# One hybrid encoder layer on one core: transposes as plain matmuls, an affine delta state, head sums in other PSUM banks, modulation sums ordered later

## The chip, the cores and the metric

The kernel runs on one core of one Trainium2 chip. The metric is the device time of one execution in microseconds (us), lower is better. A core has TensorE (PE: matmuls, with a separate row PEld for its weight loads), VectorE (DVE), ScalarE (ACT), GpSimd (POOL) and SyncE (SP, which only issues DMAs here). Each of them takes its instructions strictly in the order of the program. That order is written by a compile-time scheduler, which walks a model of the machine in time, takes the instruction of highest priority that is ready, and hands out buffers.

## The reference

One inference step of one layer (depth 1, width 1024) for two groups of rows that share the weights: 1024 prompt rows and 64 sample rows with caches.

```python
mod = (silu(c) @ w_ada + b_ada).reshape(B, 6, 1, 1024)      # shift1 scale1 gate1 shift2 scale2 gate2
h = rms_norm(x, norm_mix) * (1 + scale1) + shift1
u = h @ w_in                                                # 2568 columns, split into four mixers
mix = concat([conv(u), gated_deltanet(u), pool(u), stick_breaking(u)]) @ w_out
x = x + gate1 * mix
h2 = rms_norm(x, norm_ffn) * (1 + scale2) + shift2
x = x + gate2 * ((silu(h2 @ w_gate) * (h2 @ w_up)) @ w_down)
```

The gated DeltaNet works in chunks of 64 rows with one 64x64 state S for each of 4 heads. Inside a group of chunks, with everything that does not depend on S ready (u, w, attn, q, k per chunk):

```python
def step(S, xs):
    u_i, w_i, attn_i, q_i, k_i, gl = xs
    v_new = u_i - w_i @ S
    o = q_i @ S + attn_i @ v_new
    S = S * gl + k_i.T @ v_new
```

The stick-breaking mixer normalises its queries and keys per head (a sum of squares over the 64 columns of a head) before its attention.

## The kernel before

Rows are processed feature-major (features on partitions) in two halves: HA, prompt rows 0 to 511, and HB, prompt rows 512 to 1023 plus the 64 sample rows, 576 columns in two chunks of 288. For each half the program traces, in this order: `norm1`, `in_proj` (the input projection), `mixers`, `out_proj`, `ffn`. The last lines of the kernel (1166 to 1178) trace `in_proj(HA)`, `norm1(HB)`, `mixers(HA)`, `in_proj(HB)`, the rest of the modulation sums, `mixers(HB)`, `out_proj(HA)`, `ffn(HA)`, `out_proj(HB)`, `ffn(HB)`. Program order is the scheduler's priority, so PE fills what earlier parts leave free with later parts. Parts inside `tc.high_priority()` (evacuations of PSUM, norms, weight loads) come first.

Projections. Every product with a weight is done in single-pass fp32r on split operands: `load_w` (line 318) loads 512 KB of weights, ACT rounds them to `whi`, DVE subtracts to `wlo`; `gemm_fm` (340) runs three matmuls (hi*hi, hi*lo, lo*hi) per k tile into one PSUM bank per chunk, from `gemm_bank` (335). While `wide[0]` is false that is the pool `mm` with two banks. `in_proj` runs `sb_vab` (values of the attention), `gemm_out` for the DeltaNet columns, `sb_qk` (keys and queries, four tiles k0 k1 q0 q1), then `gemm_out` for the conv (4 tiles) and pool (2 tiles) columns. Results go to DRAM through buffers `ST` (four in all). HA and HB share the modulated inputs `hi`, `lo`, and `out_proj(HA)` loads the mixers' output `mixd` into the same buffers, in the order of slices 6, 7, 4, 5, 0, 1, 2, 3 (2 and 3 are the DeltaNet's, written as `mixA<-kbe`).

Head sums. `sb_qk` (393) copies a tile out of PSUM, squares it into `qksq`, and multiplies the squares by a block-diagonal of ones (`pqk`, line 407). The bank of `pqk` is `PC`, a pool of a single bank. `PC` is also the bank of the conv's means and variances (`pmu`, `pvar`, lines 901 and 914) and of the pool's product (`ppl`, 1016).

DeltaNet. `delta` (856) runs two groups of four chunks per half and for HB one more group of one chunk (the sample rows). Products of 64x64 blocks sit at partitions 0 to 63 and 64 to 127: `batch` (713) issues 2 pairs x chunks x 2 such matmuls, 16 in a full group. `flip` (721) transposes blocks: the lower half (hp = 0) by PE's transpose instruction (line 728), the upper half by a plain matmul with an identity. A full group has four flips: `pkt`, `pvt`, `pw0` (shown as `pw` with the operand `cst`), `pof`. The triangular inverse goes through POOL and four DRAM round trips; its result comes back as `X<-xd`. The state loop (lines 822 to 841) does for each chunk: `pvn` = w S and q S into `po`, DVE `vn`, two ACT scalings of S, `pkv` = k vn and attn vn into `po`, DVE S += `pkv`.

Modulation sums. The 16 rows of shift1 and scale1 are done at the start. The 32 others (gate1, shift2, scale2, gate2) are one DVE reduction each over a 128x1024 tile of `w_ada` (`ada_dve`, 209), once per row group. For the prompt `ada_step` (245) loads the tile into one of two buffers `g0`, `g1` (the FFN's later `th`, `tl`), behind the last weight load traced, and reduces it. `ADA_N` = 1 step is traced per projection tile of HA (12 tiles in `sb_qk` and `gemm_out`), `ADA_B` = 2 per tile of HB; line 1171 traces what is left. So 12 steps stand in HA and the other 20 in the first ten tiles of HB. `scale2` (260) needs the first 24; the last 8 (gate2) are read by the FFN's `residual`. For the sample rows `ada_sample` (253) does 32 more.

Of the kernel before, what the change touches and what calls it, by code (L numbers as in the profile page):

```python
# [7 lines left out]
F32 = mybir.dt.float32  # L8
F32R = mybir.dt.float32r
I32 = mybir.dt.int32  # L10
ACTF = mybir.ActivationFunctionType
ALU = mybir.AluOpType
# [10 lines left out]
SILU_T = 14  # L23
DEFER = 2
SHIFT_DVE = (3, 6)
ADA_N = 1
ADA_B = 2
WIDE = 6
KT = 8
FT = 22  # L30
# [29 lines left out]
def hybrid_encoder_kernel(ctx: ExitStack, tc: tile.TileContext, io):  # L60
    nc = tc.nc
    P = 128
# [39 lines left out]
    def PC(name):  # L102
        return ps_cv.tile([P, 512], F32, tag="cv", name=name)
# [9 lines left out]
    def act_(out, in_, func, bias=0.0, scale=1.0):  # L113
        nc.scalar.activation(out, in_, func, bias=bias, scale=scale)  # L114

    def copy_a(out, in_):
        nc.scalar.activation(out, in_, ACTF.Copy)  # L117
# [4 lines left out]
    def tt(out, a, b, op):  # L122
        nc.vector.tensor_tensor(out=out, in0=a, in1=b, op=op)  # L123
# [13 lines left out]
    def mm(out, lhsT, rhs, start=True, stop=True):  # L137
        return nc.tensor.matmul(out, lhsT=lhsT, rhs=rhs, start=start, stop=stop)  # L138

    def mms(out, lhsT, rhs, start=True, stop=True):  # L140
        nc.tensor.matmul(out, lhsT=lhsT, rhs=rhs, start=start, stop=stop, skip_group_check=True)  # L141
# [10 lines left out]
    def C(name):  # L152
        o, w = CONST_COLS[name]
        return cst[:, o:o + w]
# [53 lines left out]

    def ada_dve(w, col, groups):
        for g in groups:  # L210
            junk = sb.tile([P, 1024], mybir.dt.bfloat16, tag="pl", name="junk")
            nc.vector.tensor_tensor_reduce(out=junk, in0=w, in1=cbt[g], scale=1.0, scalar=V("b_ada", col),  # L212
                                           op0=ALU.mult, op1=ALU.add, accum_out=mod[:, col, g:g + 1])

# [30 lines left out]
    def ada_step(n=1):  # L245
        for _ in range(min(n, len(ada_left))):
            j = ada_left.pop(0)
            t = gp.tile([P, 1152], F32, tag=f"g{j % 2}", name="wadt")
            with behind():
                nc.sync.dma_start(out=t[:, 0:1024], in_=io["wadat"][j])  # L250
            ada_dve(t[:, 0:1024], 16 + j, (0,))
# [83 lines left out]
    def gemm_bank(name="pg"):  # L335
        turn[0] += 1
        pool, tag = BANKS[turn[0] % 8] if wide[0] else BANKS[0]
        return pool.tile([P, 512], F32, tag=tag, name=name)
# [54 lines left out]
    def sb_qk(h):  # L393
        n_ = h.n
        for pi, piece in enumerate(("k", "q")):
            for m in range(2):
                ada_step(ADA_B if h.samp else ADA_N)
                t, sq = ST("qk"), ST("qksq")
                lo = ST("qkl") if piece == "k" else t
                tiles = gemm_fm(h, io["wfm"][14 + 2 * pi + m], h.hi, h.lo, KALL)  # L400
                with tc.high_priority():
                    for ps, c0, n in tiles:
                        copy_a(t[:, c0:c0 + n], ps[:, 0:n])
                        act_(sq[:, c0:c0 + n], ps[:, 0:n], ACTF.Square)
                    for c0, n in h.chunks:
                        pn = PC("pqk")
                        mm(pn[:, 0:n], C("bdones"), sq[:, c0:c0 + n])
                        act_(sq[:, c0:c0 + n], pn[:, 0:n], ACTF.Ln, bias=epst, scale=1.0 / 64)
                    act_(sq[:, 0:n_], sq[:, 0:n_], ACTF.Exp, scale=-0.5)
                    stt(t[:, 0:n_], t[:, 0:n_], gqk[:, pi:pi + 1], sq[:, 0:n_], ALU.mult, ALU.mult)  # L410
                    copy_a(sq[:, 0:n_].bitcast(F32R), t[:, 0:n_])
                    d = sbd[piece, h.name]
                    if piece == "k":
                        nc.sync.dma_start(out=io["sbk"][m, :, h.row0:h.row0 + n_], in_=t[:, 0:n_])
                    tt(lo[:, 0:n_].bitcast(F32R), t[:, 0:n_], sq[:, 0:n_], ALU.subtract)
                    for x, v in enumerate((sq, lo)):
                        if piece == "k":
                            for y in range(2):
                                nc.sync.dma_start(out=d[2 * m + y, 64 * x:64 * x + 64], in_=v[64 * y:64 * y + 64, 0:n_])
                        else:  # L420
                            nc.sync.dma_start(out=d[128 * m:128 * m + 128, x], in_=v[:, 0:n_])
# [265 lines left out]
    def dn_group(h, feats, gate, D, ch0, nch, tok0, mtok0, S):  # L687
# [7 lines left out]
        def v4(t):  # L695
            return t[:, 0:w].rearrange("p (a c d) -> p a c d", a=2, c=nch)
# [10 lines left out]
        def PS(name):  # L707
            return PD(name)
# [12 lines left out]
        def flip(out, lhs):  # L721
            for pair in range(2):
                for c in range(nch):
                    j = (pair * nch + c) * 64
                    for hp in range(2):
                        r = slice(64 * hp, 64 * hp + 64)
                        if hp == 0:
                            nc.tensor.transpose(out[r, j:j + 64], lhs(pair, c, j)[r], C("sel2")[r, 0:64])
                        else:
                            mm(out[r, j:j + 64], lhs(pair, c, j)[r], C("sel2")[r, 0:64])  # L730

        blk = lambda t: (lambda pair, c, j: t[:, j:j + 64])
        ft = lambda i: (lambda pair, c, j: ftok(i, pair, c))
# [83 lines left out]
        batch(pwt, blk(kbe), blk(Y))  # L817
        wT = T4("X")
        copy_a(wT[:, 0:w], pwt[:, 0:w])
        po = ps_dn.tile([P, 512], F32, tag="dn", name="po")  # L820
        u4, o4 = v4(u), v4(po)
        for c in range(nch):
            pv2 = PS("pvn")
            for pair in range(2):
                j = (pair * nch + c) * 64
                for hp in range(2):
                    r = slice(64 * hp, 64 * hp + 64)
                    mm(pv2[r, pair * 64:pair * 64 + 64], wT[r, j:j + 64], S[r, pair])
                    mms(po[r, j:j + 64], qd[r, j:j + 64], S[r, pair], c == 0 and pair == 0, False)
            vn = dn.tile([P, 2, 64], F32, tag="vn", name="vn", bufs=2)  # L830
            tt(vn, u4[:, :, c], pv2[:, 0:128].rearrange("p (a d) -> p a d", a=2), ALU.subtract)
            for pair in range(2):
                act_(S[:, pair], S[:, pair], ACTF.Copy, scale=D["gl"][:, pair, ch0 + c:ch0 + c + 1])
            pk2 = PS("pkv")
            for pair in range(2):
                j = (pair * nch + c) * 64
                for hp in range(2):
                    r = slice(64 * hp, 64 * hp + 64)
                    mm(pk2[r, pair * 64:pair * 64 + 64], kup[r, j:j + 64], vn[r, pair])
                    mms(po[r, j:j + 64], at[r, j:j + 64], vn[r, pair], False, True)  # L840
            tt(S, S, pk2[:, 0:128].rearrange("p (a d) -> p a d", a=2), ALU.add)
        sq = T4("Y")
        act_(sq[:, 0:w], po[:, 0:w], ACTF.Square)
        ss = sm.tile([P, 2, 4], F32, tag="oss", name="oss")
# [323 lines left out]
    norm1(HB)  # L1168
    mixers(HA)
    in_proj(HB)  # L1170
    while ada_left:
        ada_step()
    scale2(0)
    mixers(HB)
    out_proj(HA)
    ffn(HA)
    out_proj(HB)
    ffn(HB)
# [176 lines left out]
```

## Time and profile before

| | us |
|---|---|
| three timed runs | 1528.47, 1529.11 (median), 1538.52 |
| profiled execution, whole | 1532.56 |
| its span in the trace | 1530.8 |
| PE busy, DVE busy, ACT busy in the span | 1459.6, 1030.5, 663.2 |

The profiled execution was 1.8 us longer than its span and 3.4 us longer than the median. Times in the views are counted from the start of the span. "Busy" PE time has modelled ends (matmuls are pipelined), so a busy PE is not PE at its peak rate. An engine with `q` (SPq, POOLq) is its sequencer, which issues DMAs. In a row of the timeline the columns are start, duration, engine, line, operation, out<-in, shape, count, and in brackets the idle time before it and what ended it.

### The profile page before, as it was taken

To read this page: it belongs to the slowest core of one execution; us is meant where nothing else is said; L and a number is where in the kernel's file an instruction comes from. 1 tells how busy PE (TensorE), PEld (TensorE's weight loads), DVE (VectorE), ACT (ScalarE), POOL (GpSimd) and SP (SyncE) were. 2 spreads that over 40 slices of the span, in tenths; PEclk is the share of its full clock that TensorE was granted. 3 is DMA by queue.
4 is the path that set the end of the run, shared out by engine and by line. 5 is a ranking of instruction groups with operands and counts; after the bars stand their busy time and mean duration, and the time that the engine had idled before them with its cause. 6 is when DMAs were issued, how large, how long until landed. Compare 5 with 4: busy or idle time off the path is not lost.

```text
span 1530.8 us, 24538 instructions
## 1 busy us (share of the span) xinstructions
PE 1459.6 (95%) x9688; PEld 1259.9 (82%) x9688; DVE 1030.5 (67%) x1816; ACT 663.2 (43%) x1191; POOL 88.3 (6%) x196
## 2 busy tenths in 40 slices
PE   7899999958998989999999999999999999999999
PEld 5777799835896857677878778789899999999998
DVE  7877999865379997666766588744655555555554
ACT  4446554645454567466676442222432222222221
POOL 0000400030003000200300000000000000000000
PEclk7999999968897999699999999999999999999999
DMA  8796677432354213252323477622322222222222
GB/s 287 262 295 208 207 223 236 121 75 90 117 178 145 70 45 93 82 153 84 107 91 91 131 268 260 210 95 86 135 70 84 83 83 84 83 83 84 83 84 103
DMA packets 106867, 205.41 MB, mean 134 GB/s; under 512 B 39360, under 2 KB 49024, under 8 KB 106752
## 3 DMA queue, kind: packets, MB, share of 16 engines
q1 hardware_dynamic: 99936, 193.36, 39.1%
q0 software_dynamic: 6816, 10.49, 3.1%
q8 instruction: 76, 1.25, 0.3%
q14 instruction: 39, 0.32, 0.1%
HBM read 175.57 MB, written 28.24 MB: 133 GB/s over the span
## 4 chain that ended last, share of the span: by engine, by line
PE 70%; issue 11%; DMA 7%; DVE 6%; POOL 3%; ACT 2%; SPq 1%; DVEq 0%; POOLq 0%; ACTq 0%
PE pg L138 59%; PE psC L141 2%; POOL fst L135 1%; POOL fsu L135 1%; PE pw L138 1%; DVE junk L212 1%; PE psO L141 1%; PE z L141 1%; DVE wlo L123 1%; DMA out_sbk_dram<-qk 1%; DMA wadt<-in_wadat_dram 1%; DMA X<-xd 1%; DMA fsn<-nld 1%; DVE xA L126 1%; DVE nrm L126 1%
## 5 line engine op out<-in xcount | busy, mean ns | idle before, releaser
L138 PE MATMUL pg<-hi,whi 128*128 128x288 f32 (+1 forms) x1504 | 504.8, 336 | 7.6 <-ACT vf L117 3.3
L138 PE MATMUL pg<-hi,wlo 128*128 128x288 f32 (+1 forms) x1504 | 500.6, 334 | 4.8 <-DVE wlo L123 4.8
L138 PE MATMUL pg<-lo,whi 128*128 128x288 f32 (+1 forms) x1504 | 502.5, 334 | 1.7 <-DVE lo L126 1.6
L117 ACT ACTIVATE whi<-wraw 128x1024 fp32r<-128x1024 f32 (+2 forms) x192 | 199.7, 1041 | 488.2 <-PE pg L138 422.4
L138 PEld LDWEIGHTS pg<-hi,whi 128*128 128x128 f32 x1504 | 287.1, 191 | 35.5 <-ACT vf L117 4.1
L138 PEld LDWEIGHTS pg<-hi,wlo 128*128 128x128 f32 x1504 | 286.4, 191 | 29.9 <-DVE wlo L123 6.8
L138 PEld LDWEIGHTS pg<-lo,whi 128*128 128x128 f32 x1504 | 287.2, 191 | 27.9 <-issue 3.3
L123 DVE TENSOR_TENSOR wlo<-wraw,whi 128x1024 fp32r<-128x1024 f32 (+2 forms) x192 | 230.9, 1203 | 106.6 <-ACT whi L117 105.4
L138 PE MATMUL pg<-g,whi 128*128 128x288 f32 (+1 forms) x1056 | 253.1, 332 | 0.1
L138 PEld LDWEIGHTS pg<-g,whi 128*128 128x128 f32 x1056 | 180.0, 190 | 14.8 <-ACT acc L114 0.6
L138 PE MATMUL pg<-g,wlo 128*128 128x288 f32 (+1 forms) x528 | 173.1, 331 | 0.0
L126 DVE SCALAR_TENSOR_TENSOR xs<-pg,mod,xs 128x288 f32<-128x288 f32 (+2 forms) x288 | 106.5, 413 | 85.7 <-PE pg L138 82.5
L138 PEld LDWEIGHTS pg<-g,wlo 128*128 128x128 f32 x528 | 100.1, 190 | 7.8
L123 DVE TENSOR_TENSOR fa<-fa,pg 128x288 f32<-128x288 f32 (+1 forms) x66 | 35.0, 531 | 101.4 <-PE pg L138 98.2
L126 DVE SCALAR_TENSOR_TENSOR cy<-cvb,vec,cy 128x512 f32<-128x512 f32 (+1 forms) x120 | 94.2, 799 | 0.2
L126 DVE SCALAR_TENSOR_TENSOR xA<-pg,mod,xA 128x512 f32<-128x512 f32 x96 | 70.6, 747 | 22.8 <-PE pg L138 22.6
L212 DVE CUSTOM_DVE_ANT_0 junk<-wads,cb,vec 128x1024 bf16<-128x1024 f32 x32 | 41.0, 1282 | 17.6 <-DMA wads<-in_wadat_dram 12.8
L114 ACT ACTIVATE e<-e 128x512 f32<-128x512 f32 (+4 forms) x100 | 51.9, 519 | 0.8
L212 DVE CUSTOM_DVE_ANT_0 junk<-wadt,cb,vec 128x1024 bf16<-128x1024 f32 x32 | 41.0, 1282 | 16.3 <-DMA wadt<-in_wadat_dram 16.2
L138 PE MATMUL pg<-mixs,whi 128*128 128x288 f32 x256 | 50.9, 295 | 0.0
L114 ACT ACTIVATE zs<-zs 128x512 f32<-128x512 f32 (+4 forms) x50 | 25.7, 514 | 36.8 <-DVE zs L123 35.7
L138 PEld LDWEIGHTS pg<-mixs,whi 128*128 128x128 f32 x256 | 41.0, 188 | 0.1
(304 smaller groups left out, 1922.7 us busy)
## 6 DMA issues: line engine op xcount, KB each, us to landing
wraw<-in_wgate_dram SPq DMA_DIRECT2D x44, 512.0 KB, 3.7
wraw<-in_wup_dram SPq DMA_DIRECT2D x44, 512.0 KB, 3.8
wraw<-in_wdown_dram SPq DMA_DIRECT2D x44, 512.0 KB, 3.6
wadt<-in_wadat_dram SPq DMA_DIRECT2D x32, 512.0 KB, 5.0
wads<-in_wadat_dram SPq DMA_DIRECT2D x32, 512.0 KB, 4.5
wraw<-in_wfm_dram SPq DMA_DIRECT2D x30, 512.0 KB, 4.3
wraw<-in_wout_dram SPq DMA_DIRECT2D x16, 512.0 KB, 3.7
xA<-in_xa_dram SPq DMA_DIRECT2D x16, 256.0 KB, 6.7
```

What stands on the lines that cost most here:

```text
L114: nc.scalar.activation(out, in_, func, bias=bias, scale=scale)
L117: nc.scalar.activation(out, in_, ACTF.Copy)
L123: nc.vector.tensor_tensor(out=out, in0=a, in1=b, op=op)
L126: nc.vector.scalar_tensor_tensor(out, a, s, b, op0, op1)
L135: nc.gpsimd.tensor_tensor(out=out, in0=a, in1=b, op=op)
L138: return nc.tensor.matmul(out, lhsT=lhsT, rhs=rhs, start=start, stop=stop)
L141: nc.tensor.matmul(out, lhsT=lhsT, rhs=rhs, start=start, stop=stop, skip_group_check=True)
L212: nc.vector.tensor_tensor_reduce(out=junk, in0=w, in1=cbt[g], scale=1.0, scalar=V("b_ada", col), op0=ALU.mult, op1=ALU.add, accum_out=mod[ ...
```

## The change

- `flip`: both halves become plain matmuls with the identity.
- The state loop becomes an affine map. With w itself (`pww`; before, only its transpose `pwt` was made), M = gl I - k^T w is made for all chunks at once (`pmt`, `mt_`), and S_next = k^T u + M S is accumulated in one bank per chunk (`pst`) and copied out by ACT. The states of all chunks are kept in `Sc`; `pvn`, `vn` and `po` are then done for all chunks at once.
- `pqk` takes its bank from `gemm_bank` instead of `PC`.
- `ADA_N` = 0, `ADA_B` = 1: no sums in HA, one per tile in HB (18). The loop after `in_proj(HB)` goes on until 8 are left (6 more), and the last 8 stand after `out_proj(HA)` with high priority.
- A reduction for one row group writes its unused product over its own operand instead of the bf16 buffer `pl`.

```diff
-ADA_N = 1
-ADA_B = 2
+ADA_N = 0
+ADA_B = 1
     def ada_dve(w, col, groups):
         for g in groups:
-            junk = sb.tile([P, 1024], mybir.dt.bfloat16, tag="pl", name="junk")
+            junk = w if len(groups) == 1 else sb.tile([P, 1024], mybir.dt.bfloat16, tag="pl", name="junk")
...
                     for c0, n in h.chunks:
-                        pn = PC("pqk")
+                        pn = gemm_bank("pqk")
                         mm(pn[:, 0:n], C("bdones"), sq[:, c0:c0 + n])
...
                     for hp in range(2):
                         r = slice(64 * hp, 64 * hp + 64)
-                        if hp == 0:
-                            nc.tensor.transpose(out[r, j:j + 64], lhs(pair, c, j)[r], C("sel2")[r, 0:64])
-                        else:
-                            mm(out[r, j:j + 64], lhs(pair, c, j)[r], C("sel2")[r, 0:64])
+                        mm(out[r, j:j + 64], lhs(pair, c, j)[r], C("sel2")[r, 0:64])
...
-        po = ps_dn.tile([P, 512], F32, tag="dn", name="po")
-        u4, o4 = v4(u), v4(po)
+        pw2 = PS("pww")
+        batch(pw2, blk(Y), blk(kbe))
+        wt_ = T4("W")
+        copy_a(wt_[:, 0:w], pw2[:, 0:w])
+        gi = T4("vb")
+        tt(v4(gi), bc(D["gl"]), C("sel2")[:, 0:64].unsqueeze(1).unsqueeze(1).to_broadcast(sh4), ALU.mult)
+        pm = PS("pmt")
+        batch(pm, blk(wt_), blk(kup))
+        mt_ = T4("Y")
+        tt(mt_[:, 0:w], gi[:, 0:w], pm[:, 0:w], ALU.subtract)
+        Sc = T4("kbe")[:, 0:128 * nch].rearrange("p (c a d) -> p c a d", c=nch, a=2)
+        copy_a(Sc[:, 0], S)
+
+        def each(c):
+            for pair in range(2):
+                for hp in range(2):
+                    yield pair, slice(64 * hp, 64 * hp + 64), (pair * nch + c) * 64
...
         for c in range(nch):
-            pv2 = PS("pvn")
-            for pair in range(2):
-                j = (pair * nch + c) * 64
-                for hp in range(2):
-                    r = slice(64 * hp, 64 * hp + 64)
-                    mm(pv2[r, pair * 64:pair * 64 + 64], wT[r, j:j + 64], S[r, pair])
-                    mms(po[r, j:j + 64], qd[r, j:j + 64], S[r, pair], c == 0 and pair == 0, False)
-            vn = dn.tile([P, 2, 64], F32, tag="vn", name="vn", bufs=2)
-            tt(vn, u4[:, :, c], pv2[:, 0:128].rearrange("p (a d) -> p a d", a=2), ALU.subtract)
-            for pair in range(2):
-                act_(S[:, pair], S[:, pair], ACTF.Copy, scale=D["gl"][:, pair, ch0 + c:ch0 + c + 1])
-            pk2 = PS("pkv")
-            for pair in range(2):
-                j = (pair * nch + c) * 64
-                for hp in range(2):
-                    r = slice(64 * hp, 64 * hp + 64)
-                    mm(pk2[r, pair * 64:pair * 64 + 64], kup[r, j:j + 64], vn[r, pair])
-                    mms(po[r, j:j + 64], at[r, j:j + 64], vn[r, pair], False, True)
-            tt(S, S, pk2[:, 0:128].rearrange("p (a d) -> p a d", a=2), ALU.add)
+            pS = PS("pst")
+            for pair, r, j in each(c):
+                mms(pS[r, pair * 64:pair * 64 + 64], kup[r, j:j + 64], u[r, j:j + 64], pair == 0, False)
+            for pair, r, j in each(c):
+                mms(pS[r, pair * 64:pair * 64 + 64], mt_[r, j:j + 64], Sc[r, c, pair], False, True)
+            nxt = S if c == nch - 1 else Sc[:, c + 1]
+            copy_a(nxt, pS[:, 0:128].rearrange("p (a d) -> p a d", a=2))
+        pv2 = PS("pvn")
...
+        vn = T4("W")
+        tt(vn[:, 0:w], u[:, 0:w], pv2[:, 0:w], ALU.subtract)
+        po = PS("po")
...
     in_proj(HB)
-    while ada_left:
+    while len(ada_left) > 8:
         ada_step()
     scale2(0)
     mixers(HB)
     out_proj(HA)
+    with tc.high_priority():
+        while ada_left:
+            ada_step()
     ffn(HA)
```

## Rows read from the trace of the kernel before

**Rows 1.** The page: engines over the span; the chain that ended last, by engine.
```profile
PE 1459.6 (95%) x9688; PEld 1259.9 (82%) x9688; DVE 1030.5 (67%) x1816; ACT 663.2 (43%) x1191; POOL 88.3 (6%) x196
PE 70%; issue 11%; DMA 7%; DVE 6%; POOL 3%; ACT 2%; SPq 1%; DVEq 0%; POOLq 0%; ACTq 0%
```

**Rows 2.** Busy time by stretch: us; PE, PEld, DVE, ACT, POOL; PEclk, DMA share, GB/s.
```profile
150.00:250.00 100.00, 98.89 (x867) 86.42 (x866) 94.06 (x180) 50.22 (x105) 18.31 (x33) 0.97 0.73 220
285.00:380.00 95.00, 71.90 (x656) 49.41 (x657) 61.18 (x126) 51.49 (x111) 14.91 (x36) 0.80 0.28 74
380.00:457.00 77.00, 72.72 (x532) 66.81 (x530) 40.00 (x74) 38.72 (x81) 1.73 (x3) 0.91 0.47 150
457.00:560.00 103.00, 93.81 (x650) 71.58 (x649) 97.51 (x156) 55.10 (x101) 16.12 (x34) 0.88 0.34 101
700.00:900.00 200.00, 199.33 (x1027) 158.66 (x1027) 134.19 (x214) 122.95 (x228) 20.22 (x42) 1.00 0.39 113
```

**Rows 3.** Timeline of ACT: squares of HB's first key tile; logarithm of its head sum.
```profile
287.33 0.40 ACT L114 ACTIVATE qksq<-pg 128x288 f32<-128x288 f32 x1
...
373.03 0.50 ACT L114 ACTIVATE qksq<-pqk,epst 128x288 f32<-128x288 f32 x1 [1.12 <-PE pqk L138]
```

**Rows 4.** Tiles ppl (300 to 380) and pqk (280 to 430): min/median/max ns, first and last start.
```profile
L114 ACT ACTIVATE plm<-ppl,vec x2: 670/678/687, 362.5 to 371.2; 128x512 f32<-128x512 f32 x2
...
L138 PE MATMUL pqk<-qksq,cst x16: 403/405/849, 372.3 to 414.4; 128*128 128x288 f32 x16
```

**Rows 5.** Timeline of SP: input weights, last parts of mixA, loads for out_proj(HA), last pool tile.
```profile
310.68 0.36 SPq L321 DMA_DIRECT2D wraw<-in_wfm_dram  x1
...
393.76 0.38 SPq L854 DMA_DIRECT2D mixA<-kbe  x1
...
398.81 0.35 SPq L321 DMA_DIRECT2D wraw<-in_wfm_dram  x1
...
451.35 1.77 SPq L1049 DMA_DIRECT2D mixt<-mixA  x1
...
457.38 0.33 SPq L577 DMA_DIRECT2D uplB<-ust  x1
```

**Rows 6.** Timeline of PE: first and last rows of one flip (pof); two plain batches.
```profile
286.46 0.24 PE L728 MATMUL pof<-cst,W 64*64 64x64 f32 x1
...
289.64 0.32 PE L138 MATMUL pof<-cst,W 64*64 64x64 f32 x2
...
301.49 1.15 PE L138 MATMUL pkk<-dnf 64*64 64x64 f32 x32
302.47 1.10 PE L138 MATMUL pkq<-dnf,dnf 64*64 64x64 f32 x32
```

**Rows 7.** State loop of HA's first group on DVE; tiles S_p, nl and W by operation.
```profile
231.69 0.28 DVE L123 TENSOR_TENSOR vn<-nl,pvn 128x128 f32<-128x128 f32 x1
...
274.71 0.29 DVE L123 TENSOR_TENSOR S_p<-S_p,pkv 128x128 f32<-128x128 f32 x1 [0.38 <-PE po L141]
...
L114 ACT ACTIVATE S_p<-S_p,c_gl x32: 330/346/350, 226.7 to 707.1; 128x64 f32<-128x64 f32 x32
...
L117 ACT ACTIVATE nl<-pu x5: 278/599/608, 221.7 to 790.6; 128x512 f32<-128x512 f32 x4, 128x128 f32<-128x128 f32 x1
...
L123 DVE TENSOR_TENSOR W<-pw,cst x10: 280/686/693, 189.9 to 783.9; 128x512 f32<-128x512 f32 x8, 128x128 f32<-128x128 f32 x2
```

**Rows 8.** Tile wadt: sums, landing; waits of DVE from 56 to 180.
```profile
L212 DVE CUSTOM_DVE_ANT_0 junk<-wadt,cb,vec x32: 1271/1284/1287, 63.1 to 265.0; 128x1024 bf16<-128x1024 f32 x32
DMA to landing us min/median/max: 4.0/5.0/6.6
DVE junk L212 <- DMA wadt<-in_wadat_dram: 13.1, 6, 3.9
```

**Rows 9.** Tile mixB: last attention output of HB; reads of mixB by out_proj(HB).
```profile
L489 SPq DMA_DIRECT2D mixB<-sbo x8: 451/466/503, 587.1 to 902.8; - x8
L1049 SPq DMA_DIRECT2D mixt<-mixB x8: 326/327/327, 894.6 to 978.1; - x8
```

More of the change, by code (lines that the diff above doesn't have):

```diff
@@ new lines, in dn_group @@
+        pv2 = PS("pvn")
+        for c in range(nch):
+            for pair, r, j in each(c):
+                mm(pv2[r, j:j + 64], wT[r, j:j + 64], Sc[r, c, pair])
+        vn = T4("W")
+        tt(vn[:, 0:w], u[:, 0:w], pv2[:, 0:w], ALU.subtract)
+        po = PS("po")
+        o4 = v4(po)
+        for c in range(nch):
+            for pair, r, j in each(c):
+                mms(po[r, j:j + 64], qd[r, j:j + 64], Sc[r, c, pair], c == 0 and pair == 0, False)
+        for c in range(nch):
+            for pair, r, j in each(c):
+                mms(po[r, j:j + 64], at[r, j:j + 64], vn[r, j:j + 64], False, True)
```

## The prediction, made before any run of the changed kernel

> **What bounds the kernel now.** I read the page first. PE is busy for 95% of the span and carries 70% of the chain that ended last [rows 1], so a gain has to be PE work removed or a stretch in which PE was not doing useful work. The busy times by stretch show such a stretch [rows 2]: from 285 to 380 PE is busy for 71.9 of 95 us at a granted clock of 0.80, and DVE for only 61.2. On both sides it is different: from 150 to 250 and from 457 to 560 DVE is the full engine (94.1 of 100 and 97.5 of 103), and from 700 to 900 PE is (199.3 of 200).
>
> Then I asked what keeps PE from the input projection of HB in that stretch. SP issues the next input weights at 310.7 and no more until 398.8 [rows 5]. The timeline of ACT says why [rows 3]: the squares of the first key tile of HB are done at 287.33 + 0.40 = 287.7, but the logarithm of their head sum runs at 373.0. The head sum itself starts at 372.3, right after ACT has emptied the last `ppl` (371.2 + 0.7 = 371.9) [rows 4]. `pqk`, the conv's sums and `ppl` share one bank, and `mixers(HA)` stands ahead of `in_proj(HB)` in the program, so the head sum had to wait until the conv and the pool of HA were through. It was 372.3 - 287.7 = 84.6 us late. Behind it the four `ST` buffers and both `mm` banks are held, and with them all projections. I call this the hole. The waits table charges nothing of it to `pqk`, because no engine stands at that instruction; it is in the order of the program.
>
> **Part by part.** The sum goes by the profiled execution (1532.6) and is lowered at the end by the 3.4 us by which the median is below it.
>
> *Head sum in a projection bank.* The bank comes from `mm`, which only projections use. If all that ran from 372.3 to the last pool tile at 457.4 [rows 4, 5] ran from 287.7 on, `in_proj(HB)` would end 84.6 us sooner, at 373. That is the upper end. Two things take from it. `out_proj(HA)` also needs `mixA`, whose last DeltaNet part is written at 393.8; its loads began at 451.4 [rows 5]. With no faster DeltaNet the gain is 451.4 - 393.8 = 57.6. And DVE was busy for 61.2 + 40.0 = 101.2 us from 285 to 457 [rows 2]; at the 94% at which it runs when full it needs 108 us and ends at 393, a gain of 64. I take 58. The lower end is 0, if something else held the projections.
>
> Against it: the head sums now take their turn in the two banks of the projections. In HA (one chunk) the next tile cannot start in the other bank until copy and square are through, about two ACT operations of 0.6 [rows 7]: 1.2 x 4 = 5 us. In HB both banks were in use anyway, and a logarithm (0.5) with two matmuls (2 x 0.4) comes in between [rows 3, 4]: 1.3 x 4 = 5 us, of which the old bank already cost a part. I take +4, bounds 0 to 10.
>
> *Flips.* One flip runs from 286.46 to 289.64 + 0.32 = 3.50 us; a full batch of 16 plain matmuls, the same count and shape, takes 1.15, and the next one starts 0.98 after it [rows 6]. So a flip gives back 2.35. There are 4 full groups with 4 flips and a sample group of a quarter: 17 x 2.35 = 40 us of PE, 21 of it in HB (9 flips). *Affine step.* The old loop had 64 matmuls in a full group, the new part has 112: three batches more, 3 x 0.98 = 2.9 us, in HB 2.25 groups x 2.9 = 6.6. HB's net is -14.6 us of PE. Where PE is full this counts whole, and from 457 to 560 DVE is fuller [rows 2], so I take -8, bounds 0 and -14.6. HA's net, 8 x 2.35 - 2 x 2.9 = -13, lies in the hole and only brings `mixA` forward; it is not counted again.
>
> The serial loop of HA's first group ran from 231.7 to 275.0, 43 us for four chunks with two DVE hops each [rows 7]; the new one has one ACT hop for each. In HA this brings the second group, and so `mixA`, forward; in HB the mixers end at 902.8 while `out_proj(HB)` reads `mixB` until 978.1 [rows 9], so it is worth nothing there. On DVE 8 x 0.285 goes and 3 x 0.686 comes, on ACT 8 x 0.346 goes and 0.6 with five copies of 0.3 (an estimate; at most 0.6) comes [rows 7]: 0.
>
> At this place the Trainium skill speaks against the change. "TensorE: Matmul & The Clock Gate", section Terms, says that the transpose mode of the weight load and matmul is four times faster for FP32. By that rule the flips would become dearer; the row of the flip says the opposite, and I keep the row. What the rule would give is the last rival below.
>
> *Sums ordered later.* Each is 1.28 us of DVE [rows 8]. Twelve leave HA: 15.4 us of DVE before about 180, and with them part of the 13.1 us in which DVE stood behind a landing tile. PE is mostly fed there, so I take -5, bounds 0 and -15. HB gets 24 instead of 20, 5.1 us of DVE that I put at +2 (0 to 5). The last eight come with high priority after the last weights of `out_proj(HA)`: 8 x 1.28 = 10.3 us of DVE just where it is 95% full and the residual and the norm wait for it. I take +6, bounds 0 to 10.3. Their loads sit on SP behind that weight load; in front of nothing but the FFN's weights. Writing the product as f32 in place of bf16: the trace has no such row; two 512-wide f32 operations take 2 x 0.686 = 1.37 against 1.28, so between 0 and 0.09 x 64 = 6 us of DVE; I take 0.
>
> The sum: 1532.6 - 58 + 4 - 8 - 5 + 2 + 6 = 1473.6; less 3.4, 1470.
>
> **The rivals.**
>
> *The hole closes half.* The freed projections and the attention, conv and pool of HA then run side by side on queues that keep their order, and `mixA` comes late: 30 us later than 393.8 if HB's 24 sums (24 x 1.28) all come before it. For it: DVE at 94% wherever both halves overlap [rows 2]. Against it: DVE has 34 us free in the hole. The first term is then 28: 1532.6 - 28 + 4 - 8 - 5 + 2 + 6 - 3.4 = 1500.
>
> *All of it.* The faster DeltaNet makes `mixA` ready by 375 (flips and loop of its two groups), the first term is 77 and the flips of HB count whole: 1532.6 - 77 + 4 - 14.6 - 5 + 2 - 3.4 = 1439. Against it: DVE would have to run at 101.2 of 95 us, unless work for HB's mixers moves behind.
>
> *The hole was hidden anyway*, because the mixers of HB are the real bound. Then only the small terms stay: 1532.6 + 4 - 8 - 5 + 2 + 6 - 3.4 = 1528. Against it: the 75 us of slack in [rows 9].
>
> *Slower: the late sums hold the FFN.* The eight tiles go through `g0` and `g1`, which the first two up projections of `ffn(HA)` write. Each turn is a landing (5.0) and a sum (1.28) [rows 8]: four turns, 25 us from the last output weight on. If DVE reaches the sums late, the FFN's first product cannot be stored, its `ST` buffers stay taken, and PE has only the mixers. It makes the kernel slower where the hole closes by less than these 25 us: with the first term at 0 the time is 1528 + 25 = 1553. For it: high priority puts them ahead of the norm. Against it: the norm itself takes as long.
>
> *The page's rule on transposes.* A transpose row lasts 0.24 [rows 6]; four times that is 0.96, so 8 x 0.72 = 5.8 us more for a flip and 9 x 5.8 = 52 in HB, where PE is full, in place of the 8 gained: 1470 + 8 + 52 = 1530. By the Trainium skill's rule this would be the outcome; the batch of plain FP32 blocks at 1.15 us in the trace makes it very unlikely.
>
> **How the numbers follow.** A measurement of this kernel tells about 1% (15 us) from no change. Forecast 0.52 (1470, own range 1450 to 1490), half 0.25 (1500), all 0.12 (1439), hidden 0.05 (1528), slower 0.04 (1553), the rule 0.02 (1530). Faster by over 1% means below 1514: 0.52 + 0.12 + nine tenths of 0.25 = 0.87. Within 1%: 0.05 + 0.02 + the rest of the half = 0.09. Slower 0.04. The range goes down to 1434, to take in all but the edge of the best case, and up to 1512, which leaves out the last three rivals and the tail of the half.
>
> **What the changed profile would show.** Right: the logarithm of HB's first head sum within a few us of its squares; no gap of 88 us between input weights; loads for `out_proj(HA)` before 400; the whole tail of FFN and second output projection unchanged in length but some 60 us earlier; flips of about 1.1 us; no sum before 180. Wrong: the loads for `out_proj(HA)` still after 430 with the head sums early (then `mixA` or DVE is the bound); a PE gap at the start of `ffn(HA)` ended by a sum (the slower rival); flips above 3.5 us. The forecast fails in its main term if PE stays idle between 300 and 380 with another releaser.

## The result and the profile after

The changed kernel takes 1510.98 us (median of 9 runs, 1505.27 to 1522.6) against 1529.11 before: a ratio of 0.9892, 95% interval 0.9854 to 0.9930. By the ratio that is 16.5 us (the two medians are 18.1 us apart), where 59 were forecast. The profiled execution took 1510.97 us, its span 1509.1. In the page, PE's busy time fell by 37.5 us [rows 1], and the span by only 21.7: PE now waits longer.

```profile
PE 1422.1 (94%) x10232; PEld 1239.9 (82%) x10232; DVE 1025.7 (68%) x1797; ACT 660.5 (44%) x1184; POOL 86.0 (6%) x196
...
PE 64%; DVE 13%; DMA 11%; issue 6%; ACT 4%; SPq 1%; POOL 1%; DVEq 0%; ACTq 0%; POOLq 0%
```

The same stretches as in [rows 2] (columns: PE, PEld, DVE, ACT, POOL; then PEclk, DMA share, GB/s) show where it waits:

```profile
150.00:250.00 100.00, 95.76 (x956) 81.14 (x956) 85.81 (x147) 51.09 (x111) 3.54 (x8) 0.97 0.57 175
285.00:380.00 95.00, 81.93 (x879) 69.54 (x879) 59.59 (x109) 50.65 (x110) 5.55 (x15) 0.95 0.56 171
380.00:457.00 77.00, 68.20 (x480) 58.67 (x478) 66.80 (x134) 43.36 (x85) 14.02 (x26) 0.93 0.59 197
457.00:560.00 103.00, 83.74 (x745) 64.79 (x746) 90.39 (x130) 47.44 (x84) 5.11 (x9) 0.87 0.38 103
700.00:900.00 200.00, 186.12 (x899) 146.62 (x900) 141.68 (x222) 108.42 (x190) 17.96 (x42) 0.96 0.49 154
```

The hole has largely filled: PE busy 81.9 at a clock of 0.95, where it was 71.9 at 0.80. But from 380 to 457 PE is 4.5 us less busy than before, from 457 to 560 10.1, and from 700 to 900 13.2. So new idle time stands against the gain in three later places, though the changed kernel is further on in its work in each of them. From 457 to 560 most of it is one wait for the result of the DeltaNet's triangular inverse (3.5 us before):

```profile
PE pw L138 <- DMA X<-xd: 11.2, 1, 11.2
```

The timeline of ACT answers [rows 3], and that of PE [rows 6] (here the flip `pw0`; each of its 16 matmuls makes two records, and two of the 32 are missing):

```profile
300.99 0.41 ACT L114 ACTIVATE qksq<-pg 128x288 f32<-128x288 f32 x1
303.69 0.50 ACT L114 ACTIVATE qksq<-pqk,epst 128x288 f32<-128x288 f32 x1 [2.29 <-PE pqk L138]
```

```profile
297.67 1.14 PE L138 MATMUL pw<-cst,X 64*64 64x64 f32 x30
```

The logarithm follows its squares after 2.3 us instead of 85.3, and a flip lasts 1.14 us instead of 3.50. Both steps happened as forecast. The square itself, however, comes 13.7 us later than before (300.99 against 287.33). Tiles of the changed kernel, answering [rows 5, 8]:

```profile
L577 SPq DMA_DIRECT2D udnB<-ust x8: 326/332/426, 217.3 to 297.3; - x8
...
L1064 SPq DMA_DIRECT2D mixt<-mixA x8: 320/382/544, 413.7 to 428.0; - x8
L869 SPq DMA_DIRECT2D mixA<-kbe x2: 378/1142/1907, 246.4 to 380.1; - x2
...
L212 DVE CUSTOM_DVE_ANT_0 wadt<-wadt,cb,vec x32: 1266/1279/1335, 169.8 to 514.3; 128x1024 f32<-128x1024 f32 x32
```

`mixA` is complete by 380, close to the 375 of the prediction's best case. Yet it is read at 413.7, not before 400: it is loaded into the buffers of HB's projections, whose last tile (`uplB`) leaves at 421.4. These projections now take longer: the DeltaNet columns (`udnB`) are out at 297.3, before at 279.4. The first sum runs at 169.8, where none was expected before 180. A sum in place costs 1.28 us, as much as one into bf16.

### The profile page after: what moved, and what is told of

Its sections match the earlier page's. It is cut to its first block, busy times and chain, and to the rows that moved or that the text cites. A ratio compares the mean times of both kernels' runs of the same rounds, so it can differ in the third digit from the quotient of the medians.

```text
span 1509.1 us, 25558 instructions
## 1 busy us (share of the span) xinstructions
PE 1422.1 (94%) x10232; PEld 1239.9 (82%) x10232; DVE 1025.7 (68%) x1797; ACT 660.5 (44%) x1184; POOL 86.0 (6%) x196
## 4 chain that ended last, share of the span: by engine, by line
PE 64%; DVE 13%; DMA 11%; issue 6%; ACT 4%; SPq 1%; POOL 1%; DVEq 0%; ACTq 0%; POOLq 0%
PE pg L138 53%; DMA wadt<-in_wadat_dram 3%; DVE wlo L123 2%; PE pk L138 2%; DVE cy L126 2%; DMA wads<-in_wadat_dram 2%; PE psC L141 1%; ACT whi L117 1%; DVE dnf L126 1%; PE pv L138 1%; PE psO L141 1%; PE z L141 1%; DMA out_sbk_dram<-qk 1%; DMA mixB<-sbo 1%; PE pmod L138 1%
## 5 line engine op out<-in xcount | busy, mean ns | idle before, releaser
L138 PE MATMUL pg<-hi,whi 128*128 128x288 f32 (+1 forms) x1504 | 506.6, 338 | 12.5 <-ACT whi L117 4.4
L212 DVE CUSTOM_DVE_ANT_0 wadt<-wadt,cb,vec 128x1024 f32<-128x1024 f32 x32 | 41.0, 1281 | 22.3 <-DMA wadt<-in_wadat_dram 22.2
L212 DVE CUSTOM_DVE_ANT_0 wads<-wads,cb,vec 128x1024 f32<-128x1024 f32 x32 | 41.0, 1281 | 13.1 <-DMA wads<-in_wadat_dram 13.0
L114 ACT ACTIVATE fa<-pg 128x288 f32<-128x288 f32 (+1 forms) x52 | 22.3, 428 | 40.6 <-PE pg L138 40.5
```

## The experiments

Numbers give the order of the runs. Ratios are to the kernel before, run on the same chip. Their intervals are ±0.002 to ±0.005, so a step below some 0.006 between two of them is not established.

| flips / affine | head sums: old bank | HB's moved | both moved |
|---|---|---|---|
| old order of the sums: neither | 1 | 0.9857 (E16) | 1.0062 (E2) |
| flips | 0.9828 (E3) | 0.9712 (E11) | 0.9884 (E5) |
| flips, affine | 0.9860 (E6) | 0.9810 (E15) | 0.9964 (E4) |
| new order, sample through `pl`: flips | 0.9999 (E8) | | 0.9750 (E18) |
| flips, affine | 0.9918 (E7) | 0.9906 (E12) | 0.9836 (E1) |
| the change as it stands | | | 0.9892 |

**What the hole is worth.** E2 moves the head sums of both halves, E16 those of HB alone.

```diff
-                        pn = PC("pqk")
+                        pn = gemm_bank("pqk")                               # E2
+                        pn = gemm_bank("pqk") if h.samp else PC("pqk")      # E16
```

> The kernel before with one edit, the head sums in the projection banks. Theory A (the hole closes by this edit and DVE and the queues give most of it back later): the logarithm of HB's first head sum within 3 us of its squares, the loads for the output projection of HA at 410 to 425, and a time 15 to 30 us below before, 1499 to 1514. Theory B (without a faster DeltaNet the hole only moves, since the mixers of HA are as late as ever): loads for the output projection of HA at 440 or later and a time within 6 us of before.

Measured: 1.0062 (1.0032 to 1.0092), slower. The loads come at 422.3, as in theory A; the time is that of neither.

> The kernel before with one edit, HB's head sums alone in the projection banks: the hole is closed, and HB's norm stays behind HA's head sums. Theory A (the hole is worth what PE lost in it, 95 less 71.9 = 23 us idle and 0.20 of 71.9 = 14 us by the clock, less what comes back later): HA's projections end as before (180 us), the norm before the FFN of HA 30 to 40 us earlier than before, and a time 12 to 25 us below, ratio 0.984 to 0.992. Theory B (without the faster flips the hole's end only moves to HB's mixers, as with both halves moved, 1.0062): 0.998 or more.

Measured: 0.9857 (0.9825 to 0.9890), 22 us; theory A. The windows of E16, and its tile `mixA`:

```profile
285.00:380.00 95.00, 92.97 (x774) 76.26 (x774) 66.38 (x127) 59.81 (x129) 14.02 (x37) 0.93 0.51 140
380.00:457.00 77.00, 72.45 (x483) 58.60 (x482) 72.24 (x129) 44.95 (x99) 1.12 (x2) 0.93 0.44 144
...
850.00:910.00 60.00, 54.94 (x226) 43.18 (x225) 46.51 (x69) 21.17 (x30) 0.00 (x0) 0.94 0.73 245
```

```profile
L854 SPq DMA_DIRECT2D mixA<-kbe x2: 370/370/371, 289.3 to 426.3; - x2
```

PE is full in the hole, 93.0 of 95. The last DeltaNet part of HA slides from 393.8 [rows 5] to 426.3: the mixers of HA now share a full PE with HB's projections. The norm ahead of `ffn(HA)` comes 36.4 us earlier, and 22.7 of them are left at the last output. Its column sum in the kernel before, then in E16:

```profile
543.73 1.02 PE L138 MATMUL pn<-acc,cst 128*128 128x512 f32 x2
```

```profile
507.31 2.01 PE L138 MATMUL pn<-acc,cst 128*128 128x512 f32 x2
```

In E2 that norm is as early (508.8), but all is lost where HB's mixers end. The same window of the kernel before, then of E2, then E2's waits of PE there:

```profile
850.00:910.00 60.00, 59.33 (x265) 47.17 (x264) 42.37 (x63) 30.00 (x49) 0.00 (x0) 1.00 0.59 197
```

```profile
850.00:910.00 60.00, 34.06 (x143) 25.55 (x142) 33.80 (x54) 20.21 (x35) 0.00 (x0) 0.83 0.56 186
```

```profile
PE pg L138 <- DVE sbo L123: 18.4, 1, 18.4
```

HB's last attention output is written at 897.0, hardly before the 902.8 of [rows 9]. The FFN has run ahead and its next product waits 18.4 us for DVE to get past that attention.

**The flips.** E3 makes all plain, E9 those of HA, E10 those of HB; E5 and E11 add E2's and E16's edit to E3.

```diff
-                        if hp == 0:
+                        if hp == 0 and h.samp:         # E9; E10: not h.samp; E3: no transpose
```

> The kernel before with one edit, every flip as 16 plain matmuls. Theory A (40 us of PE go, of them 21 in HB, mostly beside other work): a flip of about 1.15 us, and a time 3 to 12 us below before, 1517 to 1526. Theory B (nothing but the hole sets the time up to the FFN, and HB's flips lie under a full PE that counts whole): 15 to 21 us below. Theory C (a hidden edit): within 3 us.

Measured: 0.9828 (0.9783 to 0.9874), 26 us: more than any theory, and more than the whole change.

> The kernel before with plain flips in the groups of HA alone (8 flips, 19 us of PE); with plain flips everywhere the ratio was 0.9828 (26 us). Theory A (the mixers of HA are on the path, since the head sum and with it the projections of HB wait for them): 12 to 20 us below before, ratio 0.987 to 0.992, the head sum of HB some 15 us earlier. Theory B (the prediction: what is saved in the hole is not to be counted): ratio 0.997 to 1.002.

Measured: 0.9927 (0.9899 to 0.9955); the head sum of HB at 356.8, 15.5 us earlier. Just short of theory A, and clear of theory B.

> The kernel before with plain flips in the groups of HB alone (9 flips, 21 us of PE). Theory A (HB's DeltaNet lies beside the FFN of HA and counts in part): 5 to 13 us below before, ratio 0.9915 to 0.997. Theory B (PE is full there and each us counts): 18 to 22 us, ratio 0.986 to 0.988. Theory C (hidden): 0.999 to 1.002.

Measured: 0.9987 (0.9963 to 1.0012): 0.0003 short of theory C's range and not clear of no change, so hidden. So 11 and 2 us alone, and 26 together: they are not terms of a sum.

> The kernel before with two edits, the flips as plain matmuls and the head sums in the projection banks; by themselves these gave a ratio to before of 0.9828 and 1.0062. Theory A (where the projections of HB run earlier, they slow the mixers of HA and with them those of HB, whose end bounds the output projection of HB; the head sums then cost whatever else is changed): the first DeltaNet output of HB later than with the flips alone by 8 us or more, and a time 6 to 16 us above the flips alone, 1511 to 1521. Theory B (with the faster flips the mixers of HA no longer mind, and the two gains add up): 1485 to 1503.

Measured: 0.9884 (0.9849 to 0.9918). Theory A: the first DeltaNet output of HB is 49.5 us later than in E3 (601.9 against 552.4). The 0.0056 by which the time is above E3 is at the edge of what can be told.

> The kernel before with plain flips and with the head sums in the projection banks for HB alone, HA's left in the old bank. With the head sums of both halves moved the ratio was 0.9884, with none 0.9828. Theory A (what the move costs are the turns in HA, where the projections hold both banks and the mixers of HA start later): 0.979 to 0.983, HA's last pool tile at 176 as with the flips alone. Theory B (the cost is that HB's projections slow the mixers of HA): 0.987 to 0.990, the second DeltaNet output of HA again 40 us or more later than with the flips alone.

Measured: 0.9712 (0.9675 to 0.9750), 1485.61 us, the lowest median of all (E13 and E18 can't be told from it); better than both theories, though the second DeltaNet output of HA is 38 us later than in E3 (409.4 against 371.4), nearly the 40 of theory B. With HB's head sums alone moved, the hole and the flips add up (22 + 26, measured 44).

**What the old bank held back.** Why does moving HA's head sums cost 26 us (E11 to E5)? The first norm of HB (`norm1(HB)`) takes one of its two column sums through the same old bank, behind HA's head sums. The timeline of PE, E11 and then E5:

```profile
71.18 0.65 PE L138 MATMUL pn<-acc,cst 128*128 128x288 f32 x2
...
140.99 0.75 PE L138 MATMUL pn<-acc,cst 128*128 128x288 f32 x2
```

```profile
71.58 1.24 PE L138 MATMUL pn<-acc,cst 128*128 128x288 f32 x4
```

E13 is E5 with that norm held, E14 is E11 with it let go, E17 is E1 with it held.

```diff
-            pn = (PD if pns else PC)("pn") if early else gemm_bank("pn")
+            pn = (PD if pns else PC)("pn") if early and not h.samp else gemm_bank("pn")   # E13, E17
+            pn = (PD if pns or h.samp else PC)("pn") if early else gemm_bank("pn")        # E14
```

> Plain flips and the head sums of both halves in the projection banks (ratio 0.9884), with one more edit: the column sums of HB's first norm go through a projection bank too, so that they can't start before HA's projections. In that run they started at 72 us, with HA's head sums in the old bank at 141. Theory N (the old bank held HB's norm back, and without it that norm takes ACT and DVE from HA's projections): HA's last pool tile back from 185 to 172 to 180 us and a ratio of 0.970 to 0.977, near the 0.9712 of the run that moved HB's head sums alone. Theory T (it is the turns of the head sums in HA's two projection banks that cost): 0.985 to 0.991.

Measured: 0.9746 (0.9697 to 0.9794).

> Plain flips and HB's head sums alone in the projection banks (ratio 0.9712), with one more edit: both column sums of HB's first norm in the DeltaNet banks, so that HA's head sums, in the old bank, no longer hold them. Theory N: the norm's sums at about 72, HA's last pool tile at 182 to 187 us instead of 175, and a ratio of 0.984 to 0.990. Theory T: within 0.003 of 0.9712.

Measured: 0.9915 (0.9888 to 0.9943). The first ratio is theory N's, the second goes its way and 0.0015 beyond; theory T falls. But N's path was wrong both times: HA's last pool tile came at 182.5 in E13 and at 171.0 in E14. POOL's timeline and the tile `mixA` show another path for E14, E11 first, then E14 (`fst` is the first step of a DeltaNet group's solve, the triangular inverse; HA's first group, then HB's):

```profile
149.41 0.70 POOL L783 COPY fst<-fsn 64x256 f32<-64x256 f32 x1 [8.43 <-DMA fsn<-nld]
...
464.14 0.39 POOL L783 COPY fst<-fsn 64x256 f32<-64x256 f32 x1 [83.88 <-DMA fsn<-nld]
```

```profile
L851 SPq DMA_DIRECT2D mixA<-kbe x2: 371/374/376, 279.5 to 409.4; - x2
```

```profile
173.78 0.46 POOL L783 COPY fst<-fsn 64x256 f32<-64x256 f32 x1 [27.03 <-DMA fsn<-nld]
...
497.66 1.20 POOL L783 COPY fst<-fsn 64x256 f32<-64x256 f32 x1 [23.62 <-DMA fsn<-nld]
```

```profile
L851 SPq DMA_DIRECT2D mixA<-kbe x2: 371/377/383, 303.4 to 439.8; - x2
```

With the norm let go, HA's first solve starts 24 us later, since its data land later. HA's last DeltaNet output is then 30.4 us later, and the norm ahead of `ffn(HA)`, which cannot run without it, slips from 491.7 to 524.3. HB's first solve, too, is 33.5 us later. Between E13 and E5 the path is another: HA's last DeltaNet output is only 4.8 us later in E5 (430.4 against 425.6), that norm 4.9 (500.4 against 495.5), and HB's last attention output 10.5 (868.3 against 857.8). What delays it there stays open.

> The changed kernel with the sample's sums through pl (ratio 0.9836), with the column sums of HB's first norm in a projection bank, behind HA's projections; the same edit gained 1.4% where HA's projections still hold 12 sums. Theory N2 (HA's projections leave DVE room for one of two works, 12 sums or HB's norm; the new order takes the sums out, so the norm has to come early): DVE falls from 89 to 66 to 72 of the 120 us from 60 to 180, and the ratio is 0.990 to 1.000. Theory N (an early norm costs as such): 0.972 to 0.979.

Measured: 0.9787 (0.9736 to 0.9838), with DVE busy for 73.4 of the 120 us, a little above N2's range. N2 falls. The ratio is in N's range, but from E1 (0.9792 to 0.9880) it can't be told apart: the early norm costs with the old order of the sums, and with the new one the runs don't tell.

**The affine step.** E6 adds it to E3, E15 to E11; E18 takes it from E1.

```diff
-        po = ps_dn.tile([P, 512], F32, tag="dn", name="po")
+        pw2 = PS("pww")
...
+            copy_a(nxt, pS[:, 0:128].rearrange("p (a d) -> p a d", a=2))
```

> The kernel before with the DeltaNet part alone, the flips as plain matmuls and the affine step; head sums and order of the sums as before. Theory A (the affine step shortens the chain of the mixers, which bounds): 3 to 12 us below the flips alone, 1493 to 1502. Theory B (it adds PE work and is hidden): 1502 to 1509. Theory C (it costs, since its batches and its additional tiles wait for buffers of the previous group): 1510 or more.

Measured: 0.9860 (0.9821 to 0.9899): theory B, no difference that can be told from E3.

> Plain flips, the affine step and HB's head sums in the projection banks, the order of the sums as before: the run with the ratio 0.9712 plus the affine step. Theory A (the affine step shortens the chain of the mixers once the hole is closed): 0.964 to 0.969. Theory B (it makes no difference or costs its three batches, as it did by 0.003 beside the open hole): 0.971 to 0.976.

Measured: 0.9810 (0.9789 to 0.9831): 15 us slower than E11, beyond both theories. HB's DeltaNet columns are out at 289.4, in E11 at 274.2, and the norm ahead of `ffn(HA)` comes at 509.0 instead of 491.7.

> The changed kernel with the sample's sums through pl (ratio 0.9836) without the affine step: plain flips, head sums of both halves, new order of the sums. Theory A (the affine step costs by its three batches and by taking PE and DVE from HB's projections, as with the old order of the sums, where it cost 0.3 to 1.0%): 0.974 to 0.981. Theory B (with the new order it gains, as beside the open hole, where 0.9999 became 0.9918): 0.988 to 0.994.

Measured: 0.9750 (0.9712 to 0.9789): theory A; the affine step costs 13 us there. Tile `mixB`, of E18 and then of E1:

```profile
L489 SPq DMA_DIRECT2D mixB<-sbo x8: 451/466/496, 542.0 to 853.4; - x8
...
L851 SPq DMA_DIRECT2D mixB<-kbe x3: 377/378/383, 576.2 to 798.6; - x3
```

```profile
L489 SPq DMA_DIRECT2D mixB<-sbo x8: 451/466/502, 566.0 to 862.0; - x8
...
L869 SPq DMA_DIRECT2D mixB<-kbe x3: 377/383/432, 554.9 to 780.0; - x3
```

The affine step (E1) brings HB's last DeltaNet output forward by 18.6 us, which had 55 us to spare before the attention's last output (798.6 and 853.4 in E18). The attention's first output comes 24 us later and its last 8.6 us later. With the head sums in the old bank and the new order of the sums the same step gains 12 us (0.9999 to 0.9918, E8 to E7), so its sign depends on its company.

**The sums.** E4 is the change with the old order, all sums through `pl`; E8 is E3 with the new order; E7 and E12 are E1 with head sums in the old bank (both halves, HA's); E1 is the change with the sample's sums through `pl`.

```diff
-            junk = w if len(groups) == 1 else sb.tile(...)
+            junk = w if groups == (0,) else sb.tile(...)      # E1, E7, E8, E12, E17, E18
```

> The changed kernel with the order of the modulation's sums, and the buffer of their product, as before the change (12 sums in the projections of HA, 8 in those of HB, the other 12 before the second scale, none late, all through pl). Theory A (the early sample sums cost 17 us, the late eight some 6, and the 12 sums that left HA gave 3 to 5): 1490 to 1500. Theory B (the order of the sums costs nothing in total): 1507 to 1515. Theory C (it is what gained): 1520 or more.

Measured: 0.9964 (0.9937 to 0.9992): theory C; the new order was part of the gain.

> The kernel before with the flips as plain matmuls and the new order of the sums (none in the projections of HA, eight late, the prompt's sums with their product in place, the sample's through pl); no affine step, head sums in their old bank. Theory A (the order of the sums gives the 10 to 20 us by which the changed kernel with and without it differ, wherever the hole is): 1488 to 1497. Theory B (it gains only where the head sums are early, since then DVE is the scarce engine between 180 and 400): 1501 to 1508.

Measured: 0.9999 (0.9978 to 1.0020): it costs 26 us where E4 against E1 said that it gains 20; neither theory.

> The changed kernel with the head sums back in their old bank and with the sample's sums through pl (as in the run that had a ratio of 0.9836); what is left of the change is the DeltaNet part and the order of the sums. Theory A (the head sums in the projection banks cost): the hole at 285 to 380 is there again, and yet the time is 5 to 15 us lower than with that run, 1488 to 1498. Theory B (beside a faster DeltaNet the head sums gain): 1510 to 1525.

Measured: 0.9918 (0.9889 to 0.9946): theory B.

> The changed kernel with the sample's sums through pl (ratio 0.9836) and HA's head sums in the old bank. Theory A (the turns in HA cost): 0.978 to 0.981. Theory B (they don't; with no sums in HA's projections PE has no wait there): 0.982 to 0.986.

Measured: 0.9906 (0.9870 to 0.9941): neither. With the new order and the affine step, moving HB's head sums alone brings nothing that can be told (E7 to E12), and it is better to move HA's too. The window of HA's projections, of E11, E5, E8, E18, E12 and E17 in turn:

```profile
60.00:180.00 120.00, 106.98 (x621) 85.19 (x621) 93.98 (x181) 69.19 (x128) 19.62 (x33) 0.96 0.74 238
```

```profile
60.00:180.00 120.00, 104.81 (x563) 81.13 (x563) 85.44 (x162) 63.92 (x115) 13.74 (x33) 0.95 0.72 229
```

```profile
60.00:180.00 120.00, 102.70 (x538) 79.95 (x536) 68.98 (x131) 60.88 (x109) 18.51 (x33) 0.94 0.61 183
```

```profile
60.00:180.00 120.00, 110.75 (x634) 87.20 (x634) 89.95 (x179) 75.99 (x141) 14.00 (x33) 0.94 0.60 185
```

```profile
60.00:180.00 120.00, 103.66 (x536) 80.58 (x534) 69.04 (x130) 62.38 (x112) 17.73 (x33) 0.92 0.60 182
```

```profile
60.00:180.00 120.00, 108.47 (x637) 83.86 (x635) 73.44 (x144) 69.84 (x126) 14.17 (x33) 0.96 0.61 188
```

With the old order, PE does less here once the norm is early (107.0 to 104.8); with the new one it does more (102.7 to 110.8). In E8 DVE has neither the 12 sums nor most of the norm and is busy for 69 of 120 us; that work then comes later, where DVE is full (101.1 of 105 us from 180 to 285). One reading is that HA's projections leave DVE room for one of the two works, which gives the signs of the table. E17 speaks against it. There the norm is held even longer than in E12 (its last column sum runs at 177.1, in E12 at 141.8) and DVE is nearly as idle (73.4 against 69.0), yet PE does 108.5 against 103.7 and the ratio is 0.0119 lower. So with the new order the move of HA's head sums gains without an early norm too; why stays open.

> The changed kernel, with only the sums of the sample's modulation writing their product into the bf16 buffer pl again (they then wait for the sample attention, as before the change). Theory A (the 17 to 18 us of lead that the changed kernel loses between 840 and 900 us go to SP, where up to four loads of sample tiles stand between two FFN weight loads): the FFN weight loads keep their earlier distance and the time falls by 10 to 18 us, to 1493 to 1501. Theory B (the lead is lost there because the mixers of HB and what hangs on them end no earlier): no change, 1507 to 1515.

Measured: 0.9836 (0.9792 to 0.9880): between the theories. SP's timeline of the changed kernel shows what theory A meant, four loads of sample tiles between two FFN weights:

```profile
836.27 0.33 SPq L321 DMA_DIRECT2D wraw<-in_wup_dram  x1
837.48 8.28 SPq L256 DMA_DIRECT2D wads<-in_wadat_dram  x4
846.57 0.33 SPq L321 DMA_DIRECT2D wraw<-in_wgate_dram  x1
848.11 8.12 SPq L256 DMA_DIRECT2D wads<-in_wadat_dram  x4
...
857.41 0.33 SPq L321 DMA_DIRECT2D wraw<-in_wdown_dram  x1
```

But from the thirteenth FFN gate load of HA to the sixteenth the changed kernel takes 83.5 us (801.4 to 884.9), E1 80.9 (795.3 to 876.2), the kernel before 65.5. Of the 8 us by which the medians differ, these loads account for about 3; the rest was there before them, and its cause stays open.

## Why the prediction was wrong

The sign was right and the time lies within the range, at its upper edge (1510.98, range to 1512); the size was not right. That the time fell within the range is in part luck: steps that the sum had far too small, or not at all, cancel. Along the runs the gain comes together as follows, each step the difference of two ratios times 1529 (the steps act on each other, and another order would share them out differently): HB's head sums -22 (E16), flips -22 (E11), HA's head sums +26 (E5), new order of the sums -20 (E18), affine step +13 (E1), the sample's sums in place +9 (not established), in all -16.

**The hole, -58 (and +4 for the turns).** This step failed twice over. It took the 393.8 at which `mixA` was complete as fixed, "the gain is 451.4 - 393.8 = 57.6". But in the hole PE was already busy for 71.9 of 95 us, with those very mixers. What PE had lost there was 95 - 71.9 = 23 us, and 0.20 of 71.9 = 14 by its clock; 37 in all, an estimate from these rows, and E16 brings the norm forward by 36 and the end by 22. That 36 and 37 agree so closely is in part luck: by the same estimate PE did 0.93 x 93.0 = 86.5 us of work in E16's hole against 0.80 x 71.9 = 57.5, which is 29 more, and 3.7 us of E16's lead stood before the hole (HA's last DeltaNet column tile at 100.3 against 104.0). With the rest of the change the head sums gave less still: 12.5 us for both halves (E7 to E1). So the first rival, the hole that closes half because `mixA` comes 30 us later, was right in size (32.5 in E16), though not because of sums: none of the 32 loads for them came after 257.7 there. And the step asked only what the head sums do to their new bank, not what leaves the old one: it let HB's first norm go, which cost 21 us (E5 against E13) and 31 (E14 against E11), as much as the hole gave. Both pairs have the old order of the sums; that it cost in the changed kernel is not shown (E17).

The Trainium skill advises to use all eight PSUM banks for the most parallelism ("Perfetto Trace Analysis", Matmul Optimizations). The runs differ at this one place: giving the norm a bank where it waits for nobody costs 0.020 (E11 to E14).

**HB's mixers "worth nothing", flips -8.** The slack of 75 us read from [rows 9], between the last write of `mixB` and its last load, wasn't there. Leads against the kernel before, in us, from the profiled executions:

| lead of | E2 | E3 | E9 | E10 | E11 | E14 | E16 | E18 | after |
|---|---|---|---|---|---|---|---|---|---|
| norm ahead of `ffn(HA)` (543.7) | 34.9 | 31.3 | 34.1 | -0.7 | 52.0 | 19.4 | 36.4 | 39.7 | 28.1 |
| last attention output of HB (902.8) | 5.8 | 36.2 | 15.5 | 17.0 | 45.9 | 54.2 | 26.3 | 49.4 | 28.1 |
| last output (1527.8) | -4.9 | 33.7 | 18.7 | 4.9 | 48.6 | 20.4 | 22.7 | 37.5 | 21.7 |

The last line follows the smaller of the two above, within some 6 us in all 19 kernels that were run beside it but E2, E4 and E5, which end 10 to 12 us behind it; these three have both halves' head sums moved, the early norm and the old order of the sums. So there are two chains, the FFN's front and HB's mixers, and an edit that shortens one alone is hidden by the other (E10 brings the mixers' end forward by 17.0, E2 the FFN's front by 34.9; the end moves by 4.9 and -4.9). So the flips, which shorten both, gained 22 to 26 us instead of 8, and the rival by which the hole is hidden "because the mixers of HB are the real bound" held for E2. HA's flips, "not counted again", gave 11 by themselves.

**The affine step, 6.6 us of PE within the -8 and otherwise 0.** Its 2.9 us of PE a group was not all that it did. With HB's head sums moved it cost 12 to 15 us (E5 to E4, E15, E18): HB's projections or attention came later (E15, E18), for a DeltaNet that had 55 us or more to spare. That it takes turns from them fits these traces, but no run tests it. With the old bank it made no difference (E6) or gained 12 us (E8 to E7).

**The sums, -5 + 2 + 6.** The late eight seem to cost less than 6: from the last weight of `out_proj(HA)` to its norm it is 37.7 us (477.9 to 515.6), before 35.3 (508.4 to 543.7). The +2 for HB had more sums slow its projections. HB's DeltaNet columns do end 17.5 us later in E8 than in E3 (293.6 against 276.1), but with fewer sums, 11 against 18, between 180 and 294; so that is not their number. What the whole order of the sums brings depends on where HA's head sums are: with them moved it gains 20 us (E5 to E18), with them in the old bank it costs 9 (E6 to E7, not established) to 26 (E3 to E8). The prediction gave it +3 anywhere.

**The flips' size and the rule on transposes** came out as the trace had said: 1.14 us against 3.50. The Trainium skill also says that logical transposes ought to use transpose rather than a standard matmul ("Perfetto Trace Analysis", Transposes); for these 64x64 FP32 blocks E3 shows the opposite, 1.7% faster without. Its flip before was half transposes and half plain matmuls, taking turns; one of transposes alone was not run, so how much was the alternation is open.

What stays open: the up to 6 us that many kernels lose beyond the smaller lead, and the 10 to 12 of E2, E4 and E5 (PE is busy for 54.9 of 60 us from 850 to 910 in E16 and for 34.1 in E2, before for 59.3); why the worth of each move depends on the order of the sums; and the part of E1 that its loads don't explain.

## What to carry to other kernels

A stretch in which the projections wait was worth at most what the bounding engine lost in it, idle time and clock, and not the distance by which the waiting work could move: the work that runs there now has to run somewhere. Before a buffer is taken off a shared rotation, list what else waits in it; such a wait may be what keeps the work in a good order. Where two chains end close together, price an edit by what it does to both; here plain flips with HB's head sums alone in the projection banks (1485.61 us) beat the change by 1.8%, and nothing else that was tried was clearly better.

## What was not expected of the hardware

The granted clock of the first 60 us, a mean over its two levels (1.2 and 2.4 GHz), was 0.86 in the profiled kernel before, 0.94 in E11 and 1.00 in E16 and the changed kernel, though the edits touch nothing that runs there but the first loads for the modulation sums and at most one sum, and PE was busy for 52 to 53 us of it each time; HA's last DeltaNet column tile is out at 104.0, 97.8, 100.3 and 99.8. A few us of any lead in the table above may be this.
